# The output projection of an encoder block by seven half-size products, with results added up in SBUF

## The chip, the cores and the metric

The kernel runs on one core of a Trainium2 chip. The metric is the device time of one execution in microseconds (us), as the median of several runs. Beside it stands one profiled execution, whose span, queues and single instructions are the source of every number here. TensorE is called PE in the profile, VectorE DVE, ScalarE ACT, GpSimd POOL, SyncE SP.

## The reference

One layer of an encoder over 1024 tokens of 1024 features. Two groups of attention heads each give 512 features per token; they are gated, put side by side, projected by `w_out`, and the result is added to the input and normalised. The part that the change touches is the last two lines:

```python
h = jnp.einsum('bsd,de->bse', x, w_in[layer])
q_a, k_a, v_a, z_a, q_b, k_b, v_b, z_b = jnp.split(h, SPLIT_POINTS, axis=-1)
y_a = neighborhood_attention(q_a, k_a, v_a, rel_pos_bias[layer])      # heads of 64
y_b = windowed_gqa_with_sink(rotary(q_b), rotary(k_b), v_b, sink_logits[layer])
mixed = jnp.concatenate([y_a * jax.nn.silu(z_a), y_b * jax.nn.silu(z_b)], axis=-1)
y = jnp.einsum('bse,ed->bsd', mixed, w_out[layer])
x = layer_norm(DEEPNORM_ALPHA * x + y, ln_gain[layer], ln_bias[layer])
```

`mixed` is 1024 x 1024 (tokens by features), `w_out` 1024 x 1024, and all values are float32.

## The kernel before

**The arithmetic.** TensorE multiplies fp16 operands. To keep float32 accuracy, each operand is scaled and written as a high and a low fp16 part (high = the value cast to fp16, low = value minus high), and a product is three matmuls: high by high, high by low, low by high. The cast is ScalarE's, the subtraction VectorE's or POOL's.

**The stages.** First the input projection with the preparation of keys, values and gates. Then attention in 128 units, each a query block of one head: scores, a bias that POOL has scaled (L901), maximum and sum (L958, L974), the division with the split into fp16 (L992, L993) into one of six `split` tiles, a transposing transfer on SP's queue from `split` to `tr` (L999), and the product with the values (L1035), which VectorE multiplies with the gate into `z` (L1046). `zt[e]`, e = 0 to 7, holds feature tile e (128 features) for all 1024 tokens; e = 4 to 7 belong to group b, which comes first, e = 0 to 3 to group a, which comes last. Between the units TensorE works off a list of fillers (`fill`): the projections of the input, and at the end the first parts of the output projection.

**The output projection.** `out_mms` (L1165) makes, for a row tile t of 128 tokens and a column half a (512 columns), 8 feature tiles times 3 split matmuls of 128x512 into one PSUM bank, 16 such banks in all. The feature tiles 4 to 7 are split as soon as group b is done (`m_queue`, steps 64 to 88) and `w_out` for them at steps 96 to 131; their products for seven row tile halves fill TensorE during the last attention units (`out_head`). The rest is `final()`: the feature tiles 0 to 3 and the other eight pieces of `w_out` are split on ScalarE, VectorE and POOL, the banks are completed, and `residual` reads each bank once (L1215), adds it to the row of x that SP has loaded, and takes the statistics (L1216). `norm` works on a row tile when both halves are there: two passes on VectorE (L1260, L1263) for the left half, one on ScalarE (L1262) and two on POOL (L1265, L1266) for the right. `norm_last` does the last row tile with narrow pieces.

**What sets the order.** Up to the end of attention each engine's instructions stand in an order that the program writes by hand (`manual_schedule`); work for ScalarE, VectorE, POOL and SP that is not urgent is put in queues (`enq`), from which each step takes some. In `final()` a scheduler orders the instructions, but for `norm_last`. An engine executes its instructions in order, so what stands first and waits holds up what is behind it.

## Time and profile before

| what | value |
|---|---|
| median of three runs | 439.41 us (439.12 to 440.09) |
| profiled execution: span | 438.2 us |
| TensorE busy | 430.6 us, 98% |
| VectorE, ScalarE, POOL busy | 347.3, 299.0, 210.3 us |
| mean granted TensorE clock | 0.997 |
| last output-projection matmul done | 430.74 us |

The profiled execution's span is 1.2 us below the median. A row of a timeline gives the start in us, the duration, the engine, the line of the kernel, the operation, and destination and sources by their names in the program; a bracket behind it gives the idle time of the engine before, and who ended it. The chain of waits is read from the end backwards: each row is what the next one waited for. L1165 is the matmul of the output projection, L1215 the read of its bank, L999 the transposing transfer, L901 the scaling of the biases.

### The profile page before, as it was taken

How to read it: one execution, taken by the hardware profiler on the slowest of the kernel's cores; microseconds unless marked ns; L12 is line 12 of the kernel's file. 1: busy time of each engine (PE TensorE's matmuls, PEld its weight loads, DVE VectorE, ACT ScalarE, POOL GpSimd, SP SyncE). 2: the span in 40 equal slices, each digit the busy share in tenths (PEclk: the TensorE clock that was granted, in tenths of full speed). 3: DMA queues.
4: the chain of work that ended last, by engine and by line, in shares of the span. 5: the costliest groups of instructions: out<-in, count | busy, mean ns of one | idle time of the engine just before them, and what ended most of it. 6: DMA issues, size and time to landing. Idle time of an engine off the chain costs nothing. (4 is left out here: it accounts for less than half of the span.)

```text
span 438.2 us, 8799 instructions
## 1 busy us (share of the span) xinstructions
PE 430.6 (98%) x2954; PEld 233.0 (53%) x2954; DVE 347.3 (79%) x898; ACT 299.0 (68%) x697; POOL 210.3 (48%) x204
## 2 busy tenths in 40 slices
...
GB/s 303 318 359 72 1 251 251 273 278 245 320 136 130 161 156 163 135 157 138 168 161 176 168 189 220 193 193 219 208 220 222 204 137 364 89 1 72 263 74 72
DMA packets 134125, 81.72 MB, mean 187 GB/s; under 512 B 101312, under 2 KB 113600, under 8 KB 133824
## 3 DMA queue, kind: packets, MB, share of 16 engines
...
q8 instruction: 23, 0.38, 0.3%
...
## 5 line engine op out<-in xcount | busy, mean ns | idle before, releaser
L404 PE MATMUL ps_pj<-xf,wh 128*128 128x512 f16 x672 | 201.2, 379 | 0.0
L404 PE MATMUL ps_pj<-xf,wl 128*128 128x512 f16 x336 | 127.5, 380 | 0.0
L404 PEld LDWEIGHTS <-wh 128*128 128x128 f16 x672 | 64.8, 98 | 75.4 <-issue 0.8
L1165 PEld LDWEIGHTS <-m 128*128 128x128 f16 x408 | 38.7, 98 | 43.7
L974 ACT ACTIVATE ps_s<-sn,nm 128x385 f32<-128x385 f32 (+3 forms) x96 | 52.1, 543 | 13.5 <-DVE nm L958 12.9
L992 ACT ACTIVATE split<-ps_s,ri 128x384 f16<-128x384 f32 (+2 forms) x96 | 48.5, 539 | 18.7 <-ACT ps_s L974 12.9
L993 DVE SCALAR_TENSOR_TENSOR split<-ps_s,ri,split 128x384 f16<-128x384 f32 (+2 forms) x96 | 52.0, 570 | 5.9 <-ACT split L992 5.0
L1165 PE MATMUL ps_s<-wo,m 128*128 128x512 f16 (+1 forms) x240 | 53.3, 374 | 0.0
L404 PEld LDWEIGHTS <-wl 128*128 128x128 f16 x336 | 32.8, 98 | 38.5 <-issue 0.3
L958 DVE CUSTOM_DVE_ANT_0 sn<-ps_s,bm,nsk 128x384 f32<-128x384 f32 (+1 forms) x64 | 39.7, 635 | 6.6 <-PE ps_s L933 6.4
L219 POOL TENSOR_SCALAR wr<-wr,wsc 128x512 f32<-128x512 f32 x26 | 22.4, 862 | 47.0 <-ACT wh L214 45.5
L901 POOL TENSOR_SCALAR bias<-bias,rsg 128x552 f32<-128x552 f32 (+1 forms) x24 | 19.2, 800 | 47.7 <-DMA bias<-in_bias 34.4
L958 DVE CUSTOM_DVE_ANT_0 sn<-ps_s,bias,sg 128x264 f32<-128x264 f32 (+1 forms) x64 | 34.0, 544 | 3.4 <-POOL bias L901 1.9
L933 PE MATMUL ps_s<-ks,qs 64*128 64x384 f16 (+4 forms) x384 | 33.0, 305 | 0.0
L220 POOL TENSOR_TENSOR wl<-wr,wh 128x512 f16<-128x512 f32 x26 | 31.8, 1224 | 2.2
L1222 ACT ACTIVATE sd<-mv,eps 128x1 f32<-128x1 f32 x8 | 2.4, 295 | 41.5 <-DVE mv L1220 39.2
L1265 POOL TENSOR_TENSOR xr<-xr,gb 128x512 f32<-128x512 f32 x7 | 11.2, 1607 | 36.0 <-ACT xr L1262 36.0
L993 DVE SCALAR_TENSOR_TENSOR split<-px,ri,split 128x384 f16<-128x384 f32 (+2 forms) x32 | 24.7, 771 | 2.1 <-ACT split L992 1.9
L933 PEld LDWEIGHTS <-qs 64*128 64x128 f16 x384 | 16.1, 94 | 19.1 <-issue 13.0
L681 PEld LDWEIGHTS <-xf 128*128 128x128 f16 x216 | 21.0, 98 | 8.6 <-DVE xf L535 0.4
L1165 PE MATMUL ps_pj<-wo,m 128*128 128x512 f16 (+1 forms) x120 | 24.2, 347 | 0.0
L681 PE MATMUL ps_s<-wf,xf 128*128 128x320 f16 x144 | 23.8, 299 | 0.0
...
## 6 DMA issues: line engine op xcount, KB each, us to landing
...
```

Source lines behind the costliest of these rows:

```text
L219: nc.gpsimd.tensor_scalar(raw, raw, scale, 1.0, op0=ALU.mult, op1=ALU.mult)
L220: nc.gpsimd.tensor_sub(l, raw, h)
L404: nc.tensor.matmul(ps, a[:, k % 4, :], mv, start=(k == 0 and i == 0), stop=(k == KT - 1 and i == 2))
L681: nc.tensor.matmul(ps[:, :320], lh[t // 4, k][:, 128 * (t % 4):128 * (t % 4) + 128], rh[k][:, 320 * a:320 * a + 320], start=(k == first an ...
L901: op = enq("pool", lambda: nc.gpsimd.tensor_scalar(bv, bv, rsg, -1.0, op0=ALU.mult, op1=ALU.mult), ld, prio=0)
L933: nc.tensor.matmul(st[u, "ps"][:, :m], *parts[i], start=i == 0, stop=i == 2)
L958: nc.vector.tensor_tensor_reduce(sn[:, :m], ps[:, :m], bias_t, sg[:, c:c + 1], init, op0=ALU.add, op1=ALU.min, accum_out=nm)
L974: nc.scalar.activation(pt[:, :m], sn[:, :m], AF.Exp, bias=nm, scale=-1.0, accum_out=sm)
L992: nc.scalar.activation(hl[:, :m, 0, :c], src, AF.Copy, scale=ri)
L993: nc.vector.scalar_tensor_tensor(hl[:, :m, 1, :c], src, ri, hl[:, :m, 0, :c], op0=ALU.mult, op1=ALU.subtract)
L1165: nc.tensor.matmul(ps, lh[:, ts], rh[:, cs], start=(e == EO[0] and i == 0), stop=(e == EO[-1] and i == 2))
L1265: nc.gpsimd.tensor_mul(xr[:, h1], xr[:, h1], gb[:, h1])
```

## The change

The product is taken apart into 2 x 2 blocks: the tokens into two halves (row tiles t and 4 + t, t = 0 to 3), the features into group b (A11, A21: `zt[4 + i]`) and group a (A12, A22: `zt[i]`), the columns into two halves. Seven products of half size replace the eight: P1 = A11 B11, P7 = R T3, P2 = A12 B21, P6 = S2 T2, P4 = A22 N4, P5 = S1 T1, P3 = S4 B22, where R, S1, S2 and S4 are sums and differences of blocks of `mixed`, and T1, T2, T3, N4 of blocks of `w_out`. They are built in float32 on POOL and VectorE, mostly in place, and each is then split like the other operands. Every product is four row tiles of 4 x 3 matmuls of 128x512.

A result goes to more than one block of the output. P7 accumulates into the bank of P1 after ScalarE has copied that bank, to both column halves of an SBUF tile `acc` of 128x1024 (L1253); P5 and then P3 accumulate into the bank of P6, which VectorE has read each time before (`read`, L1293). x is added to `acc` by a transfer on POOL's queue that accumulates (L1237); the loads of x on SP's queue are gone. The row statistics come from the sums that `read` gives out and a ScalarE pass with Square (L1328), except for the last row tile. The pieces of `w_out` are kept in SBUF from their first load, so four loads are gone. `final()` now stands inside the hand-written order.

The core of the diff:

```diff
+    def split_op(key, src, home, w, lo_eng, *deps, prio=1):
+        def hi():
+            part[key] = home()
+            nc.scalar.copy(part[key][0], src())
+
+        def lo():
+            e = {"dve": nc.vector, "pool": nc.gpsimd}[lo_eng]
+            e.tensor_sub(part[key][1], src(), part[key][0])
+
+        o = enq("act", hi, *deps, prio=prio)
+        part_ops[key] = enq(lo_eng, lo, o, prio=prio)
+        return part_ops[key]
+
+    def m_first(i):
+        e = 4 + i
+        t = big_tile(f"m{e}", (128, 2, S), F16)
+        z1, z2 = zt[e][:, 0:512], zt[e][:, 512:S]
+        o = split_op(("A11", i), lambda: z1, lambda: (t[:, 0, 0:512], t[:, 1, 0:512]), 512, "pool")
+        o = enq("pool", lambda: nc.gpsimd.tensor_sub(z1, z2, z1), o)
+        split_op(("R", i), lambda: z1, lambda: (t[:, 0, 512:S], t[:, 1, 512:S]), 512, "pool", o)
...
+    def a_sums(i, n, prio=1, eng="dve"):
+        def add():
+            v = zt[4 + i].rearrange("p (b c) -> p b c", b=2)
+            e = {"dve": nc.vector, "pool": nc.gpsimd}[eng]
+            e.tensor_add(v, v, zt[i][:, 512:S].unsqueeze(1).to_broadcast([128, 2, 512]))
+
+        o = enq(eng, add, part_ops["R", i], prio=prio)
+        split_op(("S", i), lambda: zt[4 + i], wide(n), S, "dve", o, prio=prio)
+
+    def a_four(i, home, prio=1):
+        def sub():
+            nc.gpsimd.tensor_sub(zt[i][:, 0:512], zt[i][:, 0:512], zt[4 + i][:, 0:512])
+
+        o = enq("pool", sub, part_ops["Z", i], part_ops["S", i], prio=prio)
+        split_op(("S4", i), lambda: zt[i][:, 0:512], home, 512, "dve", o, prio=prio)
...
+    def prescale(n):
+        raw_ops[n] = enq("pool", lambda: nc.gpsimd.tensor_scalar(
+            wo_raw[n], wo_raw[n], wos, 1.0, op0=ALU.mult, op1=ALU.mult), load_ops.get(("wo", n)))
+
+    def raw_sub(n, a, b, *deps, eng="pool"):
+        def fn():
+            e = {"dve": nc.vector, "pool": nc.gpsimd}[eng]
+            e.tensor_sub(wo_raw[n], wo_raw[a], wo_raw[b])
+        raw_ops[n] = enq(eng, fn, *deps)
+
+    def b_first(i):
+        prescale(i)
+        split_op(("B11", i), lambda: wo_raw[i], wo_home(i), 512, "dve" if i == 2 else "pool", raw_ops[i])
+
+    def b_diff(i):
+        c, r = 4 + i, 9 + 2 * i
+        prescale(c)
+        prescale(r)
+        raw_sub(i, c, i, raw_ops[c], part_ops["B11", i])
+        raw_sub(c, c, r, raw_ops[r], raw_ops[i])
+        split_op(("T3", i), lambda: wo_raw[c], wo_home(c), 512, "dve" if i % 2 else "pool", raw_ops[c])
+        raw_sub(c, r, i, part_ops["T3", i])
+
+    def b_late(key, i, n, eng="dve", prio=1):
+        r = {"B21": 8 + 2 * i, "B22": 9 + 2 * i, "T1": i, "T2": 4 + i, "N4": 8 + 2 * i}[key]
+
+        def home():
+            return halves_of(late(n), 512)
+        split_op((key, i), lambda: wo_raw[r], home, 512, eng, raw_ops[r], prio=prio)
+
+    def b_four(i, eng="pool"):
+        r = 8 + 2 * i
+        raw_sub(r, r, 4 + i, part_ops["B21", i], raw_ops[4 + i], eng=eng)
...
+    PROD = {"P1": ("A11", "B11"), "P7": ("R", "T3"), "P2": ("A12", "B21"), "P6": ("S2", "T2"),
+            "P4": ("A22", "N4"), "P5": ("S1", "T1"), "P3": ("S4", "B22")}
+    CHAINED = ("P7", "P5", "P3")
+    acc, evac_ops, zbank = {}, {}, {}
+
+    def mms(prod, t, ps, es, cols=None, fresh=False):
+        a, b = PROD[prod]
+        o, w = (0, 512) if cols is None else cols
+        for i in es:
+            need(lhs_op(a, i), part_ops[b, i])
+            (ah, al), (bh, bl) = lhs(a, i), part[b, i]
+            ts = slice(128 * t, 128 * t + 128)
+            for n, (x1_, x2_) in enumerate(((ah, bh), (ah, bl), (al, bh))):
+                nc.tensor.matmul(ps[:, o:o + w], x1_[:, ts], x2_[:, o:o + w], start=((fresh or prod not in CHAINED) and i == n == 0),
+                                 stop=(i == 3 and n == 2), skip_group_check=prod in CHAINED and not fresh)
                 yield
 
-    obank = {}
-
-    def out_head(ts, es, tag, a=0):
-        for t in ts:
-            if tag == "pj":
-                obank[t, a] = new_group()
+    def x_add(t):
+        nc.gpsimd.dma_start(acc[t], x[t], accum_op=ALU.add)
+
+    def head(prod, t):
+        if prod == "P1":
+            if t < 2:
+                zbank[t] = new_group()
                 groups.append([])
-            elif tag is not None:
-                obank[t, a] = bank(tag)
-        for e in es:
-            for t in ts:
-                yield from out_mms(t, a, obank[t, a], [e])
+            else:
+                zbank[t] = bank("s")
+        else:
+            need(evac_ops[t])
+        yield from mms(prod, t, zbank[t], range(4))
+        n = t if prod == "P1" else 4 + t
+
+        def out():
+            acc[n] = big.tile([128, D], F32, tag="xa" if prod == "P1" else "xd", name=f"acc{n}")
+            nc.scalar.activation(acc[n].rearrange("p (b c) -> p b c", b=2),
+                                 zbank[t].unsqueeze(1).to_broadcast([128, 2, 512]), AF.Copy, scale=oinv)
+
+        evac_ops[n] = enq("act", out, prio=0)
+        enq("pool", lambda: x_add(n), evac_ops[n], prio=0)
+
+    ybank = {}
...
+        a_pair(3, 2)
+        a_sums(2, 2)
+        a_sums(3, 4)
+        for i in range(4):
+            b_late("T2", i, i % 2)
+        for i in range(4):
+            b_four(i)
+        for i in range(3):
+            b_late("N4", i, 3)
+        xbank = {}
+
+        def read(t, a, ps, o=0, w=512, accum=True):
+            xv = acc[t][:, 512 * a + o:512 * a + o + w]
+            nc.vector.scalar_tensor_tensor(xv, ps[:, o:o + w], oinv, xv, op0=ALU.mult, op1=ALU.add,
+                                           accum_out=sums[:, 2 * t + a:2 * t + a + 1] if accum else None)
+
+        def run(prod, t, ps, es=range(4), cols=None, fresh=False):
+            list(mms(prod, t, ps, es, cols, fresh))
+
+        for t in range(4):
+            run("P2", t, ybank[t], (3,))
+            read(t, 0, ybank[t])
+        nc.vector.bn_stats(stats[:, 0, :], acc[3][:, 0:512])
+        for t in range(4):
+            xbank[t] = bank(("pj", "s", "s", "t")[t])
+        for i in range(4):
+            for t in range(4):
+                run("P6", t, xbank[t], (i,))
+        for i in range(3, 4):
+            b_late("N4", i, 3)
+        for i in range(4):
+            b_late("T1", i, 3, "pool")
+        for t in range(4):
+            read(4 + t, 0, xbank[t], accum=False)
+        for i in range(4):
+            a_four(i, lambda: halves_of(late(3), 512))
+        for i in range(4):
+            b_late("B22", i, 3 if i < 2 else 5, "dve")
...
+            nc.scalar.activation(scratch, xr, AF.Square, bias=nm, accum_out=ss)
...
+        for t in range(4):
+            y = bank("s" if t < 3 else "pj")
+            run("P4", t, y)
+            read(4 + t, 0, y)
+            run("P5", t, xbank[t])
+            read(4 + t, 1, xbank[t])
+            if t < 3:
+                run("P3", t, xbank[t])
+                norm(4 + t)
+                read(t, 1, xbank[t])
+                norm(t)
+                if t == 0:
+                    nc.scalar.mul(ga, gb, ALPHA)
+        read(3, 1, xbank[3], *LAST[1], accum=False)
+        run("P3", 3, xbank[3], cols=LAST[0])
+        norm(7)
+        y = bank("pj")
+        run("P3", 3, y, cols=LAST[1], fresh=True)
+        pspe = bank("s")
+        nc.tensor.matmul(pspe[:, :NPE], identf, bb[:, :NPE], start=True, stop=False)
...
+        if i == 113:
+            a_pair(0, 0)
+            a_sums(0, 1)
+        if i == 118:
+            for n in range(4):
+                prescale(8 + 2 * n)
+        if i == 129:
+            uctx.close()
+            tiles["fp"] = ctx.enter_context(tc.tile_pool(name="fp", bufs=1, reuse_waits="tile"))
+            a_pair(1, 2)
+            a_pair(2, 2)
+            for n in range(4):
+                b_late("B21", n, 2)
+            a_sums(1, 2)
...
     need(*[op for q in queues.values() for op in q])
     clock["step"] = None
+    final()
     ordered.close()
-    final()
 
```

`late(n)` gives out space: n = 0 and 1 in tiles that held keys and queries, n = 2 in the pool `fp`, which is opened where the pool `up` with the six `split` tiles is closed (step 129), n = 3 in a pool opened in `final()`. `norm` is as before but for its statistics; `norm_last` is used for row tile 3.

Three places show how the order of instructions moves. The first is ScalarE at the end of attention. Before, behind the last two divisions (`split`, L992) stand splits of `w_out` (`wo`) and of `mixed` (`m`):

```order
L992 ACTIVATE split_1133<-px,ri 128x3x96
L992 ACTIVATE split_1134<-ps_s,ri 128x3x96
L1123 ACTIVATE wo_5131<-wor_2556,wos 128x512
L1123 ACTIVATE wo_5131<-wor_2619,wos 128x512
L1123 ACTIVATE wo_5153<-wor_2718,wos 128x512
L1123 ACTIVATE wo_5153<-wor_2799,wos 128x512
L1076 CAST m_5279<-z_1052 128x512
```

In the change, the copies of the banks of P1 and P7 (`acc`, L1253) stand there with the casts (L1089) between them:

```order
L1253 ACTIVATE acc_5194<-ps_pj,oinv 128x1024
L1089 CAST lt<-z_1508 128x1024
L1089 CAST lt<-z_4659 128x1024
L1089 CAST lt<-wor_2900 128x512
L1089 CAST lt<-wor_4316 128x512
L1089 CAST lt<-wos_1361 128x512
L1089 CAST lt<-wos_1441 128x512
L1089 CAST lt<-z_1184 128x1024
L1253 ACTIVATE acc_5233<-ps_s,oinv 128x1024
L1253 ACTIVATE acc_5272<-ps_s,oinv 128x1024
```

The copy of the second P1 bank comes first, then seven casts, and only then the copies of the third and fourth. The second place is POOL in the same part of the program. Before, the last low parts of `w_out` are followed by the norms:

```order
L1129 TENSOR_TENSOR wo_5294<-wor_4732,wo_5294 128x512
L1129 TENSOR_TENSOR wo_5299<-wor_4839,wo_5299 128x512
L1129 TENSOR_TENSOR wo_5307<-wor_5147,wo_5307 128x512
L1129 TENSOR_TENSOR wo_5310<-wor_5149,wo_5310 128x512
L1265 TENSOR_TENSOR xr<-xr,gb 128x512 x2
```

In the change the last transfer of x is followed by four subtractions for N4 (L1190), the low parts of T1 (`lu`, L1093) and the subtractions for S4 (L1126):

```order
L1237 DMA acc_5397<-in_x 128x1024
L1190 TENSOR_TENSOR wor_2900<-wor_2900,wor_2559 128x512
L1190 TENSOR_TENSOR wor_4316<-wor_4316,wor_2622 128x512
L1190 TENSOR_TENSOR wos_1361<-wos_1361,wor_2721 128x512
L1190 TENSOR_TENSOR wos_1441<-wos_1441,wor_2802 128x512
L1093 TENSOR_TENSOR lu<-wor_2041,lu 128x512
L1093 TENSOR_TENSOR lu<-wor_2152,lu 128x512
L1093 TENSOR_TENSOR lu<-wor_2269,lu 128x512
L1093 TENSOR_TENSOR lu<-wor_2374,lu 128x512
L1126 TENSOR_TENSOR z_1052<-z_1052,z_931 128x512
L1126 TENSOR_TENSOR z_1508<-z_1508,z_1184 128x512
L1126 TENSOR_TENSOR z_4659<-z_4659,z_1796 128x512 128x512
```

POOL has twelve operations there between x and the first norm, where it had four; the last of S4's four stands behind the rows shown. The third place is VectorE in the rounds at the end. Before, one round is a read, its statistics and a norm:

```order
L1216 BN_STATS stats<-xr 128x6
L1220 BN_AGGR mv<-stats 128x2
L1260 SCALAR_TENSOR_TENSOR xr<-xr,mv,gb 128x512
L1227 RECIPROCAL rstd<-sd 128x1
L1228 TENSOR_SCALAR rstd<-rstd 128x1
L1230 SCALAR_TENSOR_TENSOR nmr<-mv,rstd 128x1
L1263 SCALAR_TENSOR_TENSOR xr<-xr,rstd,bb 128x512
```

In the change the norm of row tile 4 ends, row tile 0 is read, and its norm follows ahead of the next two reads (row tile 5, from the banks of P4 and P5):

```order
L1338 SCALAR_TENSOR_TENSOR acc_5289<-acc_5289,rstd,bb 128x512
L1293 SCALAR_TENSOR_TENSOR acc_5138,sums<-ps_pj,oinv,acc_5138 128x512
L1325 TENSOR_SCALAR nmean<-sums 128x1
L1331 SCALAR_TENSOR_TENSOR acc_5138<-acc_5138,nmean,gb 128x512
L1333 RECIPROCAL rstd<-sd 128x1
L1334 TENSOR_SCALAR rstd<-rstd 128x1
L1336 TENSOR_TENSOR nmr<-nmean,rstd 128x1
L1338 SCALAR_TENSOR_TENSOR acc_5138<-acc_5138,rstd,bb 128x512
L1293 SCALAR_TENSOR_TENSOR acc_5331,sums<-ps_s,oinv,acc_5331 128x512 x2
```

So the read of P5's bank, for which P3 waits, now stands behind whole norms.

320 lines of the change are left out of this document (124 added, 196 removed).

## The prediction

> **What bounds the kernel now.** I read the page's busy shares and slices first, then the end of the chain of waits, then a table by stage, and last the single instructions of the engines that the change loads more.
>
> ```profile
> PE 430.6 (98%) x2954; PEld 233.0 (53%) x2954; DVE 347.3 (79%) x898; ACT 299.0 (68%) x697; POOL 210.3 (48%) x204
> 389.23 10.36 PE ps_pj L1165 x48
> ...
> 429.39 1.35 PE ps_pj L1165 x24
> 430.74 0.02 issue
> 430.76 0.36 DVE xr L1215
> ...
> 433.87 0.50 DVEq L1489
> ```
>
> TensorE is busy 98% of the 438.2 us span, and the chain of waits ends in one uninterrupted run of output-projection matmuls (line 1165). One 128x512 matmul costs 10.36 / 48 = 0.216 us. The last product is done at 430.74; from the last read of a bank (430.76) to the end of the span it is 438.2 - 430.76 = 7.44 us, which both kernels end with in nearly the same form. So matmuls taken away shorten the kernel one for one, as long as TensorE never waits.
>
> The next table has, for stretches of the span, the length, then busy time of PE, PEld, DVE, ACT and POOL, then the granted clock:
>
> ```profile
> 300.00:340.00 40.00, 40.00 (x343) 20.82 (x342) 32.96 (x105) 31.67 (x82) 22.45 (x26) 1.00 1.09 212
> ...
> 358.00:364.00 6.00, 6.00 (x48) 3.08 (x45) 0.00 (x0) 1.40 (x4) 2.81 (x5) 1.00 0.89 236
> 364.00:370.00 6.00, 6.00 (x32) 2.76 (x29) 5.87 (x6) 5.95 (x10) 6.00 (x5) 1.00 0.97 350
> 370.00:390.00 20.00, 20.00 (x95) 9.05 (x93) 11.13 (x18) 1.28 (x2) 0.38 (x1) 1.00 0.27 99
> 390.00:410.00 20.00, 20.00 (x94) 9.04 (x93) 20.00 (x43) 4.51 (x9) 10.90 (x7) 1.00 0.31 98
> 410.00:430.00 20.00, 20.00 (x110) 10.08 (x109) 12.83 (x25) 3.03 (x5) 9.40 (x8) 1.00 0.37 140
> ```
>
> TensorE is full in every stretch, but it is not alone: VectorE is full from 390 to 410 and the three helpers are full together from 364 to 370. Free room lies in 370 to 390 and on ScalarE. The change puts its work into just these stretches, and TensorE, in order, waits for it.
>
> **Matmuls removed: -10.4 us.** 7 products x 4 row tiles x 4 k tiles x 3 split terms = 336 full matmuls in place of 8 x 2 x 8 x 3 = 384. 48 x 0.216 = 10.4 us; TensorE would end at 430.74 - 10.4 = 420.3 and the span at 427.8. Everything below says how much of this is kept.
>
> **The loop at the end: VectorE sets its pace, +6.7 us.** In the last four rounds P3(t) accumulates into the bank in which P5(t) stands, so its first matmul waits for VectorE's read of that bank, and per round VectorE makes three reads and two norms. The price of a norm from the last ordinary one of before, and of the ScalarE work beside it:
>
> ```profile
> 422.10 0.75 DVE L1260 SCALAR_TENSOR_TENSOR xr<-xr,mv,gb 128x512 f32<-128x512 f32 x1
> 422.77 0.15 DVE L1227 RECIPROCAL rstd<-sd 128x1 f32<-128x1 f32 x1
> 422.96 0.15 DVE L1228 TENSOR_SCALAR rstd<-rstd 128x1 f32<-128x1 f32 x1
> 423.15 0.16 DVE L1230 SCALAR_TENSOR_TENSOR nmr<-mv,rstd 128x1 f32<-128x1 f32 x1
> 423.23 0.74 DVE L1263 SCALAR_TENSOR_TENSOR xr<-xr,rstd,bb 128x512 f32<-128x512 f32 x1
> 385.40 0.74 DVE L1215 SCALAR_TENSOR_TENSOR xr<-ps_s,oinv,xr 128x512 f32<-128x512 f32 x1
> 368.95 1.05 ACT L1238 ACTIVATE ga<-gb 128x1024 f32<-128x1024 f32 x1
> 344.44 0.19 ACT L974 ACTIVATION_READ_ACCUMULATOR ps_s<-sn,nm 128x1 f32 x1
> ```
>
> From the first scaling to the end of the second it is 423.23 + 0.74 - 422.10 = 1.87. Ahead of it stands the new mean (one small operation, 0.2) and a ScalarE square over 128x1024 for which VectorE waits: no square stands in the trace, the nearest is the pass over 128x1024, 1.05, with its accumulator read, 0.19; with two hand-offs of some 0.1 that is 1.4. A norm is 0.2 + 1.4 + 1.9 = 3.5, a read 0.66 to 0.74. A round is 3 x 0.68 + 2 x 3.5 = 9.0; TensorE needs 36 x 0.216 = 7.8. So after the first such read the loop runs at 9.0 a round. From the last read of a P5 bank (t = 3) there follow that read 0.7, a narrow read 0.35, a norm 3.5, a read and its statistics of 384 columns 1.2, and the 7.44 to the end: 13.1. The span ends at s0 + 3 x 9.0 + 13.1, where s0 is the start of the first read of a P5 bank.
>
> When would s0 be, if TensorE never waited before it? Up to the last attention group the order of TensorE is that of before with the same numbers of matmuls between the groups:
>
> ```profile
> 355.93 1.11 PE ps_t L1035 x24
> 357.04 5.93 PE ps_s L1165 x27
> 362.97 1.11 PE ps_t L1035 x24
> ```
>
> The last group ends at 364.08. Then come 8 + 12 of P7, 48 of P2, 48 of P6, 12 of P4 and 12 of P5: 140 x 0.216 = 30.2, s0 = 394.4, and the span ends at 394.4 + 27.0 + 13.1 = 434.5. Of the 10.4 us the loop alone takes 6.7.
>
> **A wait ahead of the last P7 tiles: +4.6 us.** P1's banks are copied to SBUF by ScalarE (line 1253), and P7(t) may start only when its bank has been copied. For t = 2 that copy stands behind seven casts (z1, z2, four of B21, S1), and the first of those writes into space that the attention's `split` tiles held, so it waits for the last transposes that read them:
>
> ```profile
> 346.44 12.12 SPq L999 DMA_TRANSPOSE tr<-split x8
> L999 SPq DMA_TRANSPOSE tr<-split x2: 1239/1244/1248, 356.0 to 357.3; - x2
> ...
> DMA to landing us min/median/max: 2.8/2.8/2.8
> 356.11 1.14 ACT L1121 CAST wo<-wor 128x512 f16<-128x512 f32 x2
> ```
>
> The last is issued at 357.3 and lands 2.8 later, 360.1. Casts cost 1.05 for 1024 columns and 1.14 / 2 = 0.57 for 512. 360.1 + 3 x 1.05 + 4 x 0.57 + 1.1 for the copy = 366.6. TensorE would be there 4 matmuls before the last group, 362.97 - 0.86 = 362.1: it waits 4.5 to 4.6, and the last attention group queues behind it. In before this wait did not exist, and its waits of TensorE there come to
>
> ```profile
> PE ps_t L1035 <- DMA tr<-split: 0.2, 1, 0.2
> ```
>
> If the transposes land as early as the casts could begin (355), the wait is nothing; if SyncE issues them 2 us later, 6.6. I take 4.6 by the rows. s0 is then 399.0.
>
> **Sums and splits between ScalarE, VectorE and POOL: +2.9 us, and +2.5 for their shared path.** P3 needs S4 and B22, the last in the line. POOL's order is: eight accumulating transfers of x, four subtractions for N4, the four low parts of T1, four for S4. Prices are
>
> ```profile
> 364.54 1.70 DVE L1077 TENSOR_TENSOR m<-z,m 128x512 f16<-128x512 f32 x1
> 366.15 1.64 DVE L1129 TENSOR_TENSOR wo<-wor,wo 128x512 f16<-128x512 f32 x1
> 373.38 2.49 DVE L1077 TENSOR_TENSOR m<-z,m 128x512 f16<-128x512 f32 x4
> 364.53 5.85 POOL L1129 TENSOR_TENSOR wo<-wor,wo 128x512 f16<-128x512 f32 x4
> 357.03 1.16 POOL L1134 TENSOR_TENSOR wo<-wor,wo 128x512 f16<-128x512 f32 x1
> 425.63 1.27 POOL L1266 TENSOR_TENSOR xr<-xr,bb 128x512 f32<-128x512 f32 x1
> ```
>
> VectorE's subtraction is 2.49 / 4 = 0.62 when POOL is idle, 1.64 beside POOL; POOL's is 1.16 (to half precision) or 1.27 alone, 5.85 / 4 = 1.46 beside VectorE. Followed without that loss: P7 ends at 373.1 after its wait; the copy of acc7 at 374.4 (ScalarE, 1.1), the casts of z3, z6, z7 in turn with VectorE's adds and low parts (1.15 for 1024 columns, about two of 0.62) to 382.5; then four casts of T2 and four of N4, 8 x 0.57 = 4.6, to 387.0, and the first of T1 at 387.6. POOL follows with 4 x 1.16 and 4 x 1.3: 397.4. The cast of the last S4 0.6, four of B22 0.56 each, and the last low part: 401.3, and VectorE's next is the read: s0 = 401.9, 2.9 after TensorE's 399.0. The eight transfers of x have no row (before loads x by SyncE); their issue on POOL lies before 375.5 behind the copies, and at anything up to 1 us each it moves nothing here.
>
> With the shared path: every VectorE operation of two SBUF operands that gets in ahead of one of the eight POOL operations holds it up by 0.62. About four do (low parts of N4 and S4): +2.5. Bounds: 0, and, if everything on the two engines from 375 to 402 is strictly one after the other, twelve POOL operations x 1.27 = 15.2 less the 7 us in which VectorE has nothing else there: +8.2.
>
> The Trainium skill, page SBUF — State Buffer, section Who interferes with whom, says that a VectorE instruction with two SBUF inputs and a GpSimd instruction that reads SBUF exclude each other. The trace agrees as far as it goes: 1.64 beside POOL against 0.62. Taken strictly it gives the +8.2 in place of +2.5.
>
> **Earlier, during attention: 0, bounds 0 and +4.** The differences of the weights (line 1184 and 1190, four times two scalings and three subtractions, about 20 us of POOL in all) go into the stretch from 300 to 340, where POOL has 22.45 of 40 busy. POOL's bias scalings are queued behind, and VectorE waits for those already:
>
> ```profile
> 346.84 0.52 DVE L958 CUSTOM_DVE_ANT_0 sn<-ps_s,bias,sg 128x288 f32<-128x288 f32 x1 [1.36 <-POOL bias L901]
> ```
>
> Next late would be the transposes and with them the wait of the last part. Their queue on SyncE runs without a gap from 346.44, so 1 to 3 us are absorbed; I take nothing.
>
> **Sum.** 438.2 - 10.4 + 6.7 + 4.6 + 2.9 + 2.5 = 444.5. The median of the runs of before is 439.41, 1.2 above the profiled span, so 445.7 for the changed kernel, 1.4% slower.
>
> **The rivals.**
> - *No stall, faster: 435.7.* The copies of P1 come in time, the helpers keep up with TensorE, and only the loop at the end is lost: 434.5 + 1.2. For it: VectorE is idle from 358 to 364 and ScalarE almost from 370 on (1.28 of 20), so there is room. Against it: the order on each queue is fixed, and the copy stands behind the casts. It decides if the transposes land before 356.
> - *Only the stall: 440.3.* The wait of 4.6 is paid, but POOL's tail is hidden: 439.1 + 1.2, no change or a little above.
> - *POOL and VectorE strictly in turn: 451.4.* 438.2 - 10.4 + 6.7 + 4.6 + 2.9 + 8.2 = 450.2, + 1.2. For it stand the four operations of 1.64; against it, that most of VectorE's reads there take one operand from PSUM.
>
> **How the numbers follow.** Forecast 0.44, with a range of its own of 442 to 449; no stall 0.25; only the stall 0.16, half of it within 0.2% of before (0.2%, or 0.9 us, is what a measurement of this kernel tells from no change), a small part below; strictly in turn 0.15. Faster 0.27, same 0.08, slower 0.65. The range is 434.5 to 453: below the no-stall case with its loop at 8.7 a round, above the strict case with 1.5 us of late transposes.
>
> **What would show it.** Right: TensorE idle for 4 to 5 us just ahead of P7's third tile, released by ScalarE's copy; gaps in each of the last rounds, released by VectorE's read; rounds of about 9 us; VectorE low parts above 1 us beside POOL; the first P5 read near 404. Wrong: TensorE idle for less than 4 us in all after 350 (then it is faster), rounds at 8 us, or waits in attention by the biases. A granted clock below 1 behind the 4.6 us gap, as the last stretch of before has it (0.80 from 430 to 439, TensorE busy 2.13 of 9), would add to the matmuls that follow and isn't in the sum.
>
> ```profile
> 430.00:439.00 9.00, 2.13 (x18) 1.11 (x14) 4.07 (x10) 1.12 (x3) 0.00 (x0) 0.80 0.17 59
> ```

## The result, and the profile of the changed kernel

The changed kernel takes 468.41 us (median of four runs, 466.91 to 469.94) against 439.61 (439.12 to 440.09) for the kernel before: a ratio of 1.065, 95% interval 1.061 to 1.069, slower. The forecast was slower by 1.4%; it is slower by 6.5%. The profiled execution of the changed kernel has a span of 465.4 us, that of before 438.2: 27.2 to explain.

First the page of the changed kernel, its busy times and the clock of TensorE in 40 slices:

```profile
PE 431.8 (93%) x2894; PEld 231.7 (50%) x2894; DVE 364.9 (78%) x923; ACT 327.3 (70%) x735; POOL 250.6 (54%) x239
PEclk9999999999999999999999999999869979999997
```

TensorE has 60 matmul rows fewer and is yet busy 1.2 us longer (430.6 before). The 48 removed matmuls should have made this -10.4, so the other matmuls took 11.6 longer. The second line shows most of the reason: the granted clock, which before fell only in the last slice, now also falls in two stretches, near the end of attention and at the start of the last part (a slice is 11.6 us: 326 to 349 and 372 to 384). TensorE was busy for 15.9 us in the four stretches in which the clock stood at 0.50, and for none of it before; half of that, 8.0, is an estimate of what the clock cost. The other 3.6 us no run takes apart. TensorE's idle time grew from 438.2 - 430.6 = 7.6 to 465.4 - 431.8 = 33.6, by 26.0. So 27.2 = 26.0 of waits + 11.6 of longer matmuls - 10.4 of removed ones.

Where the waits are is seen in a table by stage of the changed kernel (length; then busy time of PE, PEld, DVE, ACT, POOL; granted clock, DMA share, GB/s):

```profile
300.00:320.00 20.00, 20.00 (x172) 10.46 (x171) 17.03 (x50) 17.89 (x45) 16.71 (x19) 1.00 1.14 221
320.00:340.00 20.00, 15.21 (x103) 7.44 (x103) 13.56 (x39) 12.50 (x31) 19.75 (x20) 0.86 0.92 191
340.00:350.00 10.00, 9.57 (x62) 4.64 (x60) 9.72 (x21) 5.01 (x13) 8.40 (x8) 0.77 0.23 45
362.00:386.00 24.00, 17.15 (x127) 8.80 (x124) 10.81 (x20) 13.15 (x20) 4.54 (x5) 0.86 0.80 145
```

and, for the second of these stretches, of the kernel before:

```profile
320.00:340.00 20.00, 20.00 (x172) 10.42 (x171) 16.76 (x56) 14.78 (x42) 8.46 (x10) 1.00 0.99 215
```

The first loss lies in attention, where the prediction had put nothing: TensorE idle for 4.8 of the 20 us from 320, and at half the clock from 334.3 to 344.5. The second lies from 362 to 386, the stall ahead of P7's last tiles. The groups of attention's products with the values show the size of both. The one near 317 and the last two start, before and after,

```profile
316.98 1.18 PE L1035 MATMUL ps_t<-tr,va 96*64 96x256 f16 x24
355.86 1.18 PE L1035 MATMUL ps_t<-tr,va 128*64 128x256 f16 x24
362.90 1.18 PE L1035 MATMUL ps_t<-tr,va 96*64 96x256 f16 x24
```

```profile
318.56 1.18 PE L1037 MATMUL ps_t<-tr,va 96*64 96x256 f16 x24
368.95 1.18 PE L1037 MATMUL ps_t<-tr,va 128*64 128x256 f16 x24
382.05 1.87 PE L1232 MATMUL ps_s<-wo,m 128*128 128x512 f16 x4 [6.85 <-ACT acc L1253]
383.85 1.96 PE L1037 MATMUL ps_t<-tr,va 96*64 96x256 f16 x24
```

The last group but one is 13.1 us late; 1.6 of this was lost before 317. From it to the last group it is 14.90 in place of 7.04, 7.9 more, of which 6.85 is TensorE's wait for ScalarE's copy of the third P1 bank. The rest of the way: VectorE's first read of a P5 bank, the next rounds' reads, and what ScalarE does behind the first:

```profile
423.62 0.74 DVE L1293 SCALAR_TENSOR_TENSOR acc<-ps_pj,oinv,acc 128x512 f32<-128x512 f32 x1
425.96 1.28 ACT L1330 ACT_TABLE_LOAD   x1
433.93 0.74 DVE L1293 SCALAR_TENSOR_TENSOR acc<-ps_s,oinv,acc 128x512 f32<-128x512 f32 x1
452.54 0.74 DVE L1293 SCALAR_TENSOR_TENSOR acc<-ps_t,oinv,acc 128x512 f32<-128x512 f32 x1
```

From the last group to that first read it is 423.62 - 383.85 = 39.8 us, and from it to the end 41.8. The first round takes 10.3 us, with a table load of 1.28 in it, the next two (452.54 - 433.93) / 2 = 9.3 each.

### The profile page after: what moved, and what is told of

It reads as the page before. It is cut to its first block, busy times and chain, and to the rows that moved or that the text cites. A ratio compares the mean times of both kernels' runs of the same rounds, so it can differ in the third digit from the quotient of the medians.

```text
span 465.4 us, 8757 instructions
## 1 busy us (share of the span) xinstructions
PE 431.8 (93%) x2894; PEld 231.7 (50%) x2894; DVE 364.9 (78%) x923; ACT 327.3 (70%) x735; POOL 250.6 (54%) x239
## 5 line engine op out<-in xcount | busy, mean ns | idle before, releaser
L994 ACT ACTIVATE split<-ps_s,ri 128x384 f16<-128x384 f32 (+2 forms) x96 | 48.5, 539 | 19.5 <-ACT ps_s L976 11.1
L935 PE MATMUL ps_s<-ks,qs 64*128 64x384 f16 (+4 forms) x384 | 37.0, 309 | 5.5 <-DVE split L995 3.2
L1232 PEld LDWEIGHTS <-lt 128*128 128x128 f16 x192 | 19.2, 100 | 28.2 <-issue 6.9
L995 DVE SCALAR_TENSOR_TENSOR split<-px,ri,split 128x384 f16<-128x384 f32 (+2 forms) x32 | 28.5, 890 | 5.4 <-ACT split L994 5.1
L1093 DVE TENSOR_TENSOR lt<-z,lt 128x1024 f16<-128x1024 f32 x8 | 15.2, 1914 | 17.2 <-ACT lt L1089 17.2
L994 ACT ACTIVATE split<-px,ri 128x384 f16<-128x384 f32 (+2 forms) x32 | 18.4, 576 | 10.0 <-issue 5.4
L982 DVE TENSOR_SCALAR ps_s<-sm 128x2 f32<-128x2 f32 x64 | 10.2, 159 | 16.7 <-ACT ps_s L976 15.5
L1237 POOL DMA_DIRECT2D acc<-in_x x8 | 7.1, 894 | 29.5 <-ACT acc L1253 24.7
```

What stands on the lines that cost most here:

```text
L935: nc.tensor.matmul(st[u, "ps"][:, :m], *parts[i], start=i == 0, stop=i == 2)
L994: nc.scalar.activation(hl[:, :m, 0, :c], src, AF.Copy, scale=ri)
L995: nc.vector.scalar_tensor_tensor(hl[:, :m, 1, :c], src, ri, hl[:, :m, 0, :c], op0=ALU.mult, op1=ALU.subtract)
L1093: e.tensor_sub(part[key][1], src(), part[key][0])
L1232: nc.tensor.matmul(ps[:, o:o + w], x1_[:, ts], x2_[:, o:o + w], start=((fresh or prod not in CHAINED) and i == n == 0), stop=(i == 3 and n ...
```

## The experiments

All kernels start from the changed one; ratios are against the kernel before on the same chip. The start of attention's last two groups (355.86 and 362.90 in the kernel before) tells how much of a loss lies ahead of them. Each start is from one profiled execution; in the change and the five kernels whose edits lie at the very end of attention or behind it (e3, e4, e6, e7, e10) the last group but one lies between 368.76 and 370.14, so a difference below 1.4 us says nothing.

| run | edit in a few words | last group but one | last group | median, us |
|---|---|---|---|---|
| the change | | 368.95 | 383.85 | 468.41 |
| e1_lag | T3's casts three steps later | 370.08 | 385.38 | 467.31 |
| e2_late0 | Z0 and S0 ten steps later | 364.52 | 378.97 | 465.79 |
| e9_nosub | no differences of weights | 362.80 | 377.42 | 461.99 |
| e13_third | a third of the differences later | 369.85 | 383.95 | 468.08 |
| e5_spread | differences, prescales, T3, Z0/S0 later | 363.85 | 375.90 | 461.59 |
| e3_copies | copies of P1 ahead of the casts | 370.14 | 391.30 | 479.80 |
| e6_copies_xlate | e3, transfers of x issued in the last part | 369.21 | 395.43 | 483.24 |
| e10_copies_gate | e3, transfers of x behind attention | 369.83 | 376.87 | 465.04 |
| e4_n4dve | N4's differences on VectorE | 368.90 | 383.73 | 467.34 |
| e7_loop | last rounds in another order | 368.76 | 383.58 | 465.01 |
| e8_all | e5, e6, e4 and e7 together | 364.41 | 373.15 | 450.31 |
| e11_best1 | e8 with later casts and the gate | 362.30 | 369.35 | 446.38 |
| e12_best2 | e11, differences and scalings later | 357.76 | 373.18 | 450.98 |
| e14_best3 | e12 with e13's edit, T3's low parts, e8's end | 357.63 | 368.70 | 445.47 |
| e15_best4 | e14, differences two steps earlier | 358.88 | 365.93 | 442.63 |
| e16_adds | e15, sums for S2 ahead of low parts | 359.60 | 366.64 | 445.66 |
| e17_adds_n7 | e16, end in another order | 358.31 | 365.36 | 444.64 |
| e18_apart | e17, POOL and VectorE kept apart | 357.26 | 364.31 | 440.19 |

### The delay in attention: e1, e2, e5, e9, e13

The rows of the changed kernel that the first reading rests on, from its timeline:

```profile
328.44 2.50 POOL L1190 TENSOR_TENSOR wor<-wor,wor 128x512 f32<-128x512 f32 x2
330.97 1.29 ACT L1089 CAST wo<-wor 128x512 f16<-128x512 f32 x2 [4.68 <-POOL wor L1190]
333.74 0.31 PE L935 MATMUL ps_s<-ks,qs 64*128 64x352 f16 x1 [1.93 <-DVE split L995]
335.26 2.28 PE L935 MATMUL ps_s<-ks,qs 64*128 64x352 f16 x11 [1.22 <-DVE nm L960]
339.05 4.10 DVE L1093 TENSOR_TENSOR lt<-z,lt 128x1024 f16<-128x1024 f32 x2
339.18 2.13 PE L1037 MATMUL ps_t<-tr,va 128*64 128x256 f16 x24 [1.64 <-DVE z L1048]
339.94 2.13 POOL L1190 TENSOR_TENSOR wor<-wor,wos 128x512 f32<-128x512 f32 x1
343.51 0.54 ACT L994 ACTIVATE split<-px,ri 128x288 f16<-128x288 f32 x1 [4.40 <-issue]
```

ScalarE stands 4.68 us at a cast of T3, whose difference POOL has not yet made; attention's divisions (L994) are behind it in ScalarE's order, VectorE waits for these, and TensorE for VectorE. At 339 VectorE's two low parts of Z0 and S0 (128x1024) take 4.10 beside a running POOL, with attention's VectorE work behind them, and ScalarE waits 4.40. Two causes offer themselves: POOL's lateness, and VectorE's wide low parts.

**e1_lag** puts T3's casts three steps later in ScalarE's order.

```diff
+        raw_ops[c].lag = 3
         split_op(("T3", i), lambda: wo_raw[c], wo_home(c), 512, "dve" if i % 2 else "pool", raw_ops[c])
```

> One part changed: ScalarE's cast of T3 comes three steps later in its queue behind POOL's difference of the weights, so that it no longer stands ahead of the divisions of the attention while POOL is still at work. Theory (a queue's head holds up attention: ScalarE idle 4.7 us from 326.3 to 331.0 until POOL's subtraction L1190 ends): that gap goes, the last group of attention (383.9 in the change) comes 3 to 6 us earlier and the time is about 463. Rival (POOL itself is full and its bias scalings set the pace): the wait moves to the bias, VectorE waits for POOL at L960 instead, the time stays within 1.5 us of 468.

467.31 us (ratio 1.063, 1.055 to 1.071). The wait of ScalarE doesn't go, it moves to the next product of POOL, the last prescaled piece for B11:

```profile
333.04 0.62 ACT L1089 CAST wo<-wor 128x512 f16<-128x512 f32 x1 [4.95 <-POOL wor L1184]
```

**e2_late0** moves Z0's and S0's split from step 113 to 123.

```diff
-        if i == 113:
+        if i == 123:
             a_pair(0, 0)
             a_sums(0, 1)
```

> One part moved: the pair Z0 and the sum S0 with their 1024-wide low parts on VectorE go from step 113 to step 123. Theory (the two low parts, 4.1 us from 339.05 beside POOL's subtractions, stand ahead of the row sums of attention and hold ScalarE and TensorE): the gap from 338.5 to 343.5 on ScalarE goes, 3 to 6 us less, about 464. Rival (the first gap of ScalarE behind POOL has already made everything late and this one is only the same delay seen again): under 1.5 us.

465.79 us (1.059, 1.048 to 1.071). The block of 4.10 us on VectorE is gone and the last group but one starts 4.4 us earlier; ScalarE's wait for POOL stays (5.47 at 330.67).

**e9_nosub** leaves out the twelve differences, so that its output is not the product.

```diff
-        raw_sub(i, c, i, raw_ops[c], part_ops["B11", i])
-        raw_sub(c, c, r, raw_ops[r], raw_ops[i])
...
-        raw_sub(c, r, i, part_ops["T3", i])
```

> Leaves out the twelve subtractions on POOL that build T3, T1 and N4 out of the weights (15 us of POOL between 305 and 357), so the output is not the product; all casts, low parts, scalings and matmuls stay. Theory (POOL's extra work during attention is what makes ScalarE, VectorE and so TensorE late there): TensorE's waits between 330 and 357 are under 2 us in all, its clock stays full there, and the last group of attention comes 8 to 13 us earlier than 383.9; time 455 to 460. Rival (the two 1024-wide low parts of Z0 and S0 on VectorE, which stay, make up most of it): 3 us or less earlier, 464 or more.

461.99 us (1.051, 1.044 to 1.057); the last group but one starts 6.2 us earlier and ScalarE's wait for POOL falls to 0.51. The wait ahead of P7 stays, 6.58. So the differences account for about half of the 13.1, less than the theory of the expectation and more than its rival.

**e13_third** tests the sum of POOL's work alone: the four differences that only P6 needs are taken out of the crowded stretch.

```diff
-        raw_sub(c, r, i, part_ops["T3", i])
+    def b_third(i):
+        raw_sub(4 + i, 9 + 2 * i, i, part_ops["T3", i])
...
+        if i == 134:
+            for n in range(4):
+                b_third(n)
```

> Edit: of the twelve differences of weights that POOL takes during attention, the four that only P6 needs (the third of each block) are put into the queue at step 134 instead of behind T3's parts. The output is the full product. If POOL's backlog is what delays attention, taking 4 x 1.27 = 5.1 us out of the stretch from 320 to 340 brings the last attention group from 383.9 to 379 to 381 and the span to about 461 to 463; ScalarE's 4.7 us wait for POOL shrinks or stays short. Rival, that VectorE's 1024-wide low parts at 339 alone decide: the last group stays within 1 us of 383.9. Of no effect on the wait ahead of P7 (6 to 7 us) and on the rounds.

468.08 us (1.065, 1.060 to 1.069): the expectation failed. 5 us of POOL's work less, and the cast waits longer than before:

```profile
331.62 0.62 ACT L1089 CAST wo<-wor 128x512 f16<-128x512 f32 x1 [6.63 <-POOL wor L1190]
330.33 1.26 POOL L1190 TENSOR_TENSOR wor<-wor,wor 128x512 f32<-128x512 f32 x1
```

In the changed kernel the wait ends with two differences (328.44, 2.50 us), here with one, but POOL comes to it 1.9 us later. It had stood 1.37 us just ahead of 320 for a load of biases (0.92 in the change) while work on the weights was queued behind; whether that load is the whole reason isn't shown. Taking work from POOL's total did not help, then: what the cast feels is when its own operand is ready.

**e5_spread** puts the differences at steps 106, 113, 119, 124, the prescales at 126, and takes e1 and e2 along.

```diff
-DIFF_AT = {100: 0, 105: 1, 110: 2, 115: 3}
+DIFF_AT = {106: 0, 113: 1, 119: 2, 124: 3}
```

> POOL's work for T3 spread out: the four groups of differences start at steps 106, 113, 119 and 124 in place of 100 to 115, the scalings at 126 in place of 118, the cast of T3 three steps behind, and Z0 and S0 at 123. Nothing else. Theory (POOL is behind by some 5 us near 327, whatever ScalarE casts next from it is late and holds up the attention): ScalarE's waits for POOL near 325 to 335 and TensorE's waits in attention (5 us and the slow clock behind them) go; the last group of attention comes about 13 us earlier than 383.9 and the time is near 455. Rival (the room for POOL later is as small): the wait moves 20 us later, time 462 or more.

461.59 us (1.049, 1.040 to 1.057), mean clock 0.984 in place of 0.973. The group before the last two starts at 352.49 in place of 361.69 (348.60 before), but new waits follow: 4.02 for VectorE's gate ahead of the last group but one, and 0.95 + 1.15 for T3, which now comes late.

### The wait ahead of P7: e3, e6, e10

The chain of waits of the changed kernel has a transposing transfer in it that takes 6.54, and ScalarE's casts wait for it (the first row is of the chain, the others of the timeline, the last two POOL's first transfers of x):

```profile
369.33 6.54 DMA tr<-split
375.97 1.99 ACT L1089 CAST lt<-z 128x1024 f16<-128x1024 f32 x2 [9.37 <-DMA tr<-split]
364.01 1.04 POOL L1237 DMA_DIRECT2D acc<-in_x  x1 [5.85 <-ACT acc L1253]
366.91 0.86 POOL L1237 DMA_DIRECT2D acc<-in_x  x1 [1.85 <-ACT acc L1253]
```

The prediction had taken 2.8 for that landing. **e3_copies** puts ScalarE's copies of P1 ahead of the casts (the block with Z1, Z2, B21, S1 from step 129 to 138), which should end the wait.

```diff
         if i == 129:
             uctx.close()
             tiles["fp"] = ctx.enter_context(tc.tile_pool(name="fp", bufs=1, reuse_waits="tile"))
+        if i == 138:
             a_pair(1, 2)
             a_pair(2, 2)
```

> One order changed: on ScalarE the copies of the third and fourth bank of P1 come ahead of the casts that wait for the last transposes; everything else is as in the change. Theory (TensorE waits 6.9 us for the copy of the third bank only because it stands behind those casts): the wait at P7 goes and its slow matmuls after it too, the last group of attention comes 7 to 8 us earlier; 461 if nothing new is waited for. Rival (the casts are late by the transposes anyway and P2 waits for them in place of P7): less than 3 us, with a new wait of TensorE at P2.

479.80 us (1.091, 1.080 to 1.103): much slower. The copy is early, and with it POOL's transfers of x, six of which are now issued from 365.2 to 377.9 (two in the change). The last transposes land after 20.7 us, and TensorE waits for them:

```profile
391.30 2.13 PE L1037 MATMUL ps_t<-tr,va 96*64 96x256 f16 x24 [14.04 <-DMA tr<-split]
DMA to landing us min/median/max: 2.8/3.4/20.7
```

**e6_copies_xlate** writes the transfers of x at the start of the last part instead.

```diff
-        enq("pool", lambda: x_add(n), evac_ops[n], prio=0)
...
+        for n in range(8):
+            x_add(n)
         a_pair(3, 2)
```

> As e3 (copies of P1's banks ahead of the casts), and the eight accumulating transfers of x are all issued behind the last attention group instead of one behind each copy. Theory (those transfers, 512 KB each, hold up the last transposing transfers: landing 6.5 us in the change and 14 us of TensorE's wait in e3, where more of them were in flight): the transposes land in 2.8 to 4 us, TensorE's wait ahead of the last attention group is under 2 us, that group comes about 8 us earlier than 383.9, the time is 459 to 462. Rival (the transposes are late by their queue on SyncE, not by x): the wait of 6 to 14 us stays, the time is 468 to 480.

483.24 us (1.098, 1.093 to 1.103). POOL has nothing else to do there, so it issues them at nearly the same times as in e3 (364.3, 367.2 against 365.2, 368.1); the last transposes land after 26.2 and TensorE waits 19.10. The edit did not separate what it should.

**e10_copies_gate** holds the transfers back by a tiny operation that reads the last column of attention's output.

```diff
+        gate = fp.tile([128, 1], F32, name="gate", bufs=1)
+        nc.gpsimd.tensor_scalar(gate, zt[3][:, S - 1:S], 1.0, 1.0, op0=ALU.mult, op1=ALU.mult)
+        for n in range(8):
+            x_add(n)
```

> As e3 (copies of P1's banks ahead of the casts), and POOL issues the eight accumulating transfers of x only behind a small operation that reads the last column written by attention, so none is in flight while the last transposes are. In e6 they had been moved behind nothing that waits, and were issued at the same times as in e3. Theory (accumulating transfers hold up the transposes): the last transpose lands within 4 us, TensorE's wait of 14 us ahead of the last attention group is under 2 us; that group comes near 375, and the time is 456 to 462. Rival (queue on SyncE, or the copies themselves): the wait stays above 6 us, 468 to 480.

465.04 us (1.058, 1.054 to 1.061). There is no wait at the last group or at P7, and all transposes land in time:

```profile
376.87 1.18 PE L1037 MATMUL ps_t<-tr,va 96*64 96x256 f16 x24
DMA to landing us min/median/max: 2.8/3.2/4.4
```

From the group before it is 376.87 - 369.83 = 7.04, as in the kernel before. So e3's 14.04 us was made by the transfers of x in flight. The gain is given back at P4 and P3 (waits of 1.88, 1.90 and 7.42): POOL issues the eight transfers until 398.7, and its differences for N4 stand behind them.

### The shared path and the last rounds: e4, e7

In the changed kernel a low part of S2 (128x1024, 1.23 us when POOL is idle) takes 5.02, and T2's casts queue behind it, for which TensorE waits 3.04 in P6:

```profile
394.49 2.83 POOL L1190 TENSOR_TENSOR wor<-wor,wor 128x512 f32<-128x512 f32 x2
395.82 5.02 DVE L1093 TENSOR_TENSOR lt<-z,lt 128x1024 f16<-128x1024 f32 x1 [1.11 <-ACT lt L1089]
397.03 2.71 POOL L1190 TENSOR_TENSOR wos<-wos,wor 128x512 f32<-128x512 f32 x2
403.63 0.38 PE L1232 MATMUL ps_pj<-lt 128*128 128x512 f16 x1 [3.04 <-ACT lt L1089]
```

**e4_n4dve** gives these four differences to VectorE.

```diff
         for i in range(4):
-            b_four(i)
+            b_four(i, "dve")
```

> One thing moved: the four subtractions for N4 are done by VectorE, not by POOL. Theory (VectorE and POOL exclude each other: a low part of 1.2 us took 5.0 us from 395.8 because POOL's four subtractions ran through at that time): that low part takes 1.2, TensorE's wait of 4.0 us at P6 shrinks to 1 or less, less 2.5 us that VectorE does itself: 465 to 467. Rival (P6 waits for ScalarE's casts and the order of the sums anyway): no less wait at P6, 468 to 470.

467.34 us (1.063, 1.052 to 1.074). No low part is held up there any more and the waits in P6 fall from 4.0 to 0.4, but the wait ahead of P3's first tile grows from 2.37 to 6.32:

```profile
423.70 2.72 PE L1232 MATMUL ps_pj<-lu 128*128 128x512 f16 x6 [6.32 <-DVE acc L1293]
```

**e7_loop** reorders the last rounds: P4(t + 1) between P5(t) and P3(t), a norm's ScalarE part ahead of it and its VectorE part behind, B22's low parts behind the first read of a P5 bank.

```diff
+        four(0)
         for t in range(4):
             run("P5", t, xbank[t])
             read(4 + t, 1, xbank[t])
             if t < 3:
+                norm_a(4 + t)
+                if t > 0:
+                    norm_b(t - 1)
+                four(t + 1)
                 run("P3", t, xbank[t])
-                norm(4 + t)
+                norm_b(4 + t)
                 read(t, 1, xbank[t])
-                norm(t)
+                norm_a(t)
```

> Only the end is reordered: P4 of the next row tile stands between P5 and P3 on TensorE, each norm is cut in two so that VectorE works on another row tile while ScalarE squares, and the low parts of B22 stand behind the first read of a P5 bank. Theory (VectorE waits for the square in every norm, 1.3 us twice a round, and the read that P3 needs stands behind whole norms): rounds of 7.8 to 8.2 us in place of 9.3, TensorE's waits for a read under 0.3 us a round, 4 to 6 us less: 463. Rival (VectorE's own work fills the rounds): rounds stay above 9 us, under 1 us less.

465.01 us (1.057, 1.051 to 1.063), 3.4 less than the change by the medians, 0.8 by the profiled spans (464.6). The waits of the rounds (2.37, 2.29, 1.38, 1.64 in the change) are gone but for one of 2.44; the last row tile's wait for ScalarE grows from 3.65 to 4.98. So it was the order, not VectorE's total work, that made these waits. Of this little shows in the time; the waits ahead of the loop are still there.

### All together: e8, e11, e12, e14, e15

**e8_all** joins e5 (with e1 and e2 in it), e6 (with e3), e4 and e7.

> All changes together: POOL's work spread (e5), copies first with x transferred late (e6), N4's subtractions on VectorE (e4), the reordered end (e7). If the named waits are all that the change lost, TensorE waits under 4 us after 300 and the time is 430 to 440, no slower than before. If they hide each other or a new one follows, 445 to 455.

450.31 us (1.026, 1.020 to 1.031). **e11_best1** adds the gate of e10, lets the casts of B11 and T3 wait five steps (`lag = 5`), splits Z0 and S0 at step 131, puts three of the four differences one or two steps earlier, makes T1's low parts earlier, loads ScalarE's table early and puts row tile 6's norm later, just ahead of the last row tile's reads; **e12_best2** differs from it in the steps of the differences and of the scalings behind them (128 in place of 126).

```diff
-DIFF_AT = {106: 0, 112: 1, 117: 2, 122: 3}
+DIFF_AT = {110: 0, 115: 1, 120: 2, 125: 3}
```

> Everything of e8, and: casts of B11 and T3 five steps behind POOL, Z0 and S0 at step 131, the differences at 106, 112, 117, 122, x gated as in e10, T1's low parts ahead of N4 on POOL, the last norms behind the last reads of P5, the square root's table loaded early, the small product of mean and scale with one SBUF operand. If the waits named so far are all there are, the attention ends within 3 us of its time in the kernel before (363) and the time is 434 to 440. If POOL is full in any order, attention stays 6 us late or more: 443 to 450.

> As e11, with the differences at 110, 115, 120 and 125 and the scalings at 128. If POOL's backlog near 327 is the cause, less wait there than e11; P7 then waits for T3, some 1 to 3 us. Same or 2 us either way against e11.

446.38 (1.015, 1.007 to 1.023) and 450.98 (1.026, 1.022 to 1.030). The moved norm goes with harm: the last row tile's wait for ScalarE is 7.5 in both, against 3.50 in e8 and 2.89 and 4.55 in e14 and e15, which leave it out. In e12 attention is within 1.9 us of the kernel before, but then P7 waits for T3, which POOL delivers too late:

```profile
365.60 6.79 PE L1234 MATMUL ps_pj<-wo,m 128*128 128x512 f16 x17 [5.25 <-POOL wo L1093]
```

**e14_best3** and **e15_best4** take e13's edit along, e14 with three of T3's low parts on VectorE, e15 with the differences at steps 108, 113, 118, 123.

> Edit: the kernel of e12_best2 with the third differences of weights in the queue at step 131 or later (as in e13), three of T3's four low parts on VectorE, and the end of e7/e8 (no last norms moved). If T3 is late there only because POOL has too much ahead of it, the wait of 5.25 us ahead of P7 goes (below 1 us), the last attention group starts near 366 instead of 373.2, and the span is 437 to 442. Rival, that VectorE's low parts of T3 now hold up attention: the group stays at 370 or later and the span at 445 or more.

> Edit: as e14, with the differences two steps earlier (steps 108, 113, 118, 123) and T3's low parts as in the change (two on POOL). By POOL's backlog: attention a little later than in e14 (last group 366 to 369), no wait for T3, span 439 to 444. If two steps earlier bring the crowding back: last group 369 or later, span 445 to 447, as in e11.

445.47 (1.013, 1.009 to 1.017) and 442.63 (1.011, 1.003 to 1.019). In e15 both come in time: attention is 3.0 late and nothing waits for T3. In e14 T3 still costs 1.32 + 0.72. The wait of 5.25 for T3 is thus gone with e13's edit, but other edits came with it; its own part isn't shown. One of e15's three runs took 446.37.

### One low part of 10 us: e16, e17, e18

In e15 P6 still waits 1.28 + 0.97 for T2, behind S2 and S3. **e16_adds** makes both sums before the low parts, and loads ScalarE's table later (the edit against e15):

```diff
-        a_sums(2, 2)
-        a_sums(3, 4)
+        o2, o3 = a_sums(2, None), a_sums(3, None)
+        a_pair(3, 2)
+        split_op(("S", 2), lambda: zt[6], wide(2), S, "dve", o2)
+        split_op(("S", 3), lambda: zt[7], wide(4), S, "dve", o3)
```

> Edit: the kernel of e15_best4, but in the last part both sums for S2 (1.22 each on VectorE) stand ahead of the low parts instead of between them, and the early load of ScalarE's table stands behind T2's and N4's casts instead of ahead of z3's. By the theory that the order of the helpers sets the waits, the two waits ahead of P6's last tiles (1.28 and 0.97 in e15) go, and the span falls by about 2 us, to 438 to 439.5: no difference from the kernel before that can be told. Rival, that VectorE's total work binds there: the waits come back in P5 or P3 and the span stays at 440 to 442.

445.66 us (1.013, 1.008 to 1.017), span 444.5: the rival was nearer, though by its reason (VectorE's total work) and its number (440 to 442) it isn't right either. Both waits are gone, and one of 5.78 stands inside P4(0), ahead of its last two matmuls. The timeline of e16 shows what made it:

```profile
390.68 4.81 POOL L1093 TENSOR_TENSOR lu<-wor,lu 128x512 f16<-128x512 f32 x4
390.88 10.03 DVE L1093 TENSOR_TENSOR lu<-wos,lu 128x512 f16<-128x512 f32 x1
395.14 5.20 POOL L1128 TENSOR_TENSOR z<-z,z 128x512 f32<-128x512 f32 x4
400.95 1.01 PE L1238 MATMUL ps_s<-lu,lt 128*128 128x512 f16 x2 [5.78 <-DVE lu L1093]
```

One low part of N4, 0.62 us of work, began 0.2 us behind the first of eight POOL operations, and ended at 400.91, half a microsecond behind the last. POOL's took 1.20 and 1.30 each, nearly as alone. By the medians e16 can't be told from e15, whose runs go from 442.56 to 446.37; by the waits it can. In e15 the same eight operations of POOL had not shut VectorE out:

```profile
389.69 5.16 POOL L1093 TENSOR_TENSOR lu<-wor,lu 128x512 f16<-128x512 f32 x4
393.81 1.59 DVE L1093 TENSOR_TENSOR lu<-wos,lu 128x512 f16<-128x512 f32 x1
394.81 5.85 POOL L1126 TENSOR_TENSOR z<-z,z 128x512 f32<-128x512 f32 x4
```

There the last low part of N4 took 1.59, which is one POOL operation's wait and its own work, and POOL paid with 1.46 each for S4's four.

**e17_adds_n7** moves two VectorE passes of row tile 7 behind the last row tile's.

> Edit: as e16, and the two passes of VectorE over the left half of row tile 7 stand behind the last row tile's instructions instead of ahead of its reads. They took 0.75 and 1.30 there; the last row tile's reads start about 2 us earlier, and the two passes come to 1.5 at the end, so the span should fall by 0 to 1 us against e16. Rival, that the end is set by the last transfers, which now start behind these passes: 0 to 2 us longer than e16.

444.64 us (1.010, 1.006 to 1.015), within 1 us of e16, as expected, and with the same low part of 10.04.

**e18_apart** keeps the two engines apart: T1's four low parts on VectorE, POOL's four differences for S4 held back until they are done, and S4's splits behind the first read of a P5 bank (the edit against e17).

```diff
-            b_late("T1", i, 3, "pool")
...
+        for i in range(4):
+            b_late("T1", i, 3)
+        nc.gpsimd.tensor_scalar(gate, part["T1", 3][1][:, 511:512], 1.0, 1.0, op0=ALU.mult, op1=ALU.mult)
```

> Edit: the kernel of e17_adds_n7, but POOL and VectorE are kept apart in time in the last part: T1's four low parts go from POOL to VectorE, POOL's four differences for S4 are held back by a tiny operation that reads the last of them, and S4's splits stand behind the first read of a P5 bank. In e16 and e17 one low part of 128x512 on VectorE began 0.2 us behind POOL's run of eight operations and took 10.03 us. By the theory that a VectorE operation on two SBUF operands does not get through while POOL's operations follow each other, this one now takes 0.62, the wait of TensorE ahead of P3(0) (5.80 in e17) falls to 1 to 2.5, and the span to 439.5 to 441. Rival, that VectorE's total work binds there: the wait stays at 4 or more and the span at 443 to 444.

440.19 us, twelve runs, against 439.79: ratio 1.001, interval 0.9995 to 1.0028, no difference. The low parts take 0.62 again, VectorE's reads of PSUM banks run beside POOL's four differences at 0.74, P4(0) runs without a wait (the expectation speaks of P3(0); the rows of e16 have the wait inside P4(0)), and P3(0) waits 0.8 in two pieces. From the timeline, the page and the table by stage of e18:

```profile
388.56 2.49 DVE L1093 TENSOR_TENSOR lu<-wor,lu 128x512 f16<-128x512 f32 x4
391.38 4.96 POOL L1328 TENSOR_TENSOR z<-z,z 128x512 f32<-128x512 f32 x4
395.21 0.74 DVE L1305 SCALAR_TENSOR_TENSOR acc<-ps_s,oinv,acc 128x512 f32<-128x512 f32 x1
396.55 0.69 DVE L1093 TENSOR_TENSOR lu<-z,lu 128x512 f16<-128x512 f32 x1
...
PE 422.2 (97%) x2894; PEld 228.0 (52%) x2894; DVE 366.8 (84%) x931; ACT 326.7 (75%) x736; POOL 245.1 (56%) x233
...
320.00:340.00 20.00, 20.00 (x172) 10.40 (x171) 17.34 (x51) 15.01 (x41) 18.10 (x20) 1.00 1.03 206
```

POOL is busy 18.10 of 20 us from 320 to 340, nearly as in the change (19.75), and TensorE is full there at full clock. TensorE's busy time is 422.2, 8.4 below the kernel before: here the removed matmuls show. Its idle time is 436.7 - 422.2 = 14.5, 6.9 more than before, and eats most of them.

## Why the prediction was wrong

The direction held, the size did not: 465.4 against 444.5 for the span. Taken by the prediction's own steps:

- **Earlier, during attention: 0, bounds 0 and +4. This is the step that failed**: 13.1. The text itself had the numbers against it, 22.45 us of POOL's 40 taken and about 20 more put in, but it looked for the price at POOL's own next readers, the biases. The readers that decided were ScalarE's casts: they stand in ScalarE's order at the step where POOL's result was planned, and attention's divisions stand behind them. e9 shows it: without the differences the cast's wait falls to 0.51 and attention gains 6.2. That the cast's place alone would cure it isn't shown: three steps later did not help (e1), nor did less work for POOL (e13). VectorE's wide low parts of Z0 and S0 are the other part (e2: 4.4). It is not POOL's total alone: in e18 POOL is busy for 48.6 us from 300 to 362, against 51.9 in the change, and attention runs 1.4 us late, with the casts five steps later, the differences eight, a third of them later still, and Z0 and S0 at step 131. Which of these edits gives how much, no run shows. Of the 13.1 us, 1.6 had been lost before 317; TensorE's idle time is 4.8 (320 to 340) + 0.4 (340 to 350) + 1.1 (350 to 362) = 6.3; an estimate of the clock's share is 3.8, half of the 7.6 us for which TensorE was busy at 0.50; 1.4 is not pinned down.
- **A wait ahead of the last P7 tiles: +4.6, bounds 0 and 6.6.** Mechanism, place and releaser are right; the wait is 6.85, and with the slow matmuls behind it 7.9. The term that was mis-sized is the landing of the last transposes, 6.5 in place of 2.8, because the transfers of x were in flight (e3 20.7, e6 26.2, e10 at most 4.4). The prediction had looked only at what their issue costs POOL, and had said that it moves nothing.
- **Sums and splits +2.9, shared path +2.5 (0 to 8.2).** From the last attention group to the first P5 read it is 39.8 against 394.4 - 363.0 = 31.4 without waits: 8.4 in place of 5.4. Of the 8.4, 4.0 are the two waits in P6 (3.04 and 0.96), 1.5 lie just ahead of that read, and 2.9 are longer matmuls. That the two engines exclude each other is right, the form and the place were not. The prediction let VectorE get in ahead of POOL and hold it up by 0.62 at S4 and B22; in this run POOL's four operations shut VectorE out (5.02 in place of 1.23) at S2, and T2 was late for P6. Less the 2.9 for the sums, 5.5 is left, between the forecast 2.5 and the strict case's 8.2; that it lies inside the bounds is luck, since it arose at another place and is in part the longer matmuls.
- **The loop at the end: +6.7.** Rounds of 9.0 were forecast; they take 10.3, 9.3 and 9.3, and 12.9 from the last P5 read to the end (13.1 forecast). Missing was the table load, 1.28, in the first round. That VectorE's dependent norms set the pace is right for this order; e7 shows that it is the order's doing.
- **Matmuls removed: -10.4.** Right, but visible only where TensorE does not wait (e18: -8.4).
- **The clock** was named as something that "isn't in the sum". It is a term of the sum: an estimate of 8.0 of the 11.6 us by which the matmuls were longer, nearly as large as the whole gain. Where the waits go, it goes with them (mean clock 0.973 in the change, 0.984 in e5, 0.990 in e18).

The four differences, 13.1 + (7.9 - 4.6) + (8.4 - 5.4) + (41.8 - 40.1), come to 21.1; the span missed by 20.9. Of the rivals, none had a delay in attention; "only the stall", 440.3, is what e18 comes to after many edits of the order, but by luck: e18 has no stall ahead of P7.

No version that was run beats the kernel before. What stays open is whether e18's remaining idle time, 14.5 us, of which 3.0 is the last row tile's wait for ScalarE and 2.4 the last P3's for VectorE, can be ordered away too.
